# Four one-bank sums, memory attention in row pairs, another order of gates and of weight splits, in an encoder step on one core

## The chip, the cores and the metric

The kernel runs on one core of one Trainium2 chip. The metric is the device time of one execution in microseconds (us). A core has TensorE (PE in the rows: matmuls; PEld is its load of weights), VectorE (DVE), ScalarE (ACT), GpSimd (POOL) and SyncE (SP, which issues most DMAs). TensorE writes its sums to PSUM, eight banks of 512 floats per partition; VectorE and ScalarE read them from there.

## The reference, cut to what matters

One step of a one-layer encoder for 512 prompt rows and 32 sample rows, 544 columns in all in the kernel, width 1024. Three branches are computed from the normalised input, each is projected, gated and added up; then an output projection and a SwiGLU feed-forward part follow:

```python
h = rms_norm(x, norm_mix)
q, k, v, xb, gb, qc = split(h @ w_in)
a_out = diff_attention(q, k, v, ...)                    # 8 heads
b_out = rglru_branch(xb, gb, ...)                       # conv, gates, linear recurrence, gelu
c_out = cross_attention(qc, mem_k, mem_v)               # "memory attention": 4 heads, 256 memory rows
gates = sigmoid(h @ w_gate + b_gate)                    # three of them
merged = gates[0]*(a_out @ w_proj_a) + gates[1]*(b_out @ w_proj_b) + gates[2]*(c_out @ w_proj_c)
x = x + merged @ w_out
h2 = rms_norm(x, norm_ffn)
g_ff, u_ff = split(h2 @ w_ffn_in)
x = x + (silu(g_ff) * u_ff) @ w_ffn_out
```

The memory keys and values, `mem_k` and `mem_v`, are outputs too (`o_mk`, `o_mv`).

## The kernel before

Everything is kept transposed: features on partitions, the 544 rows of the input as columns, in two halves of 272 (`HT`). Each float32 operand is split into a high and a low part (`wh`, `wl` of the weights, `hh`, `hl` of the input), and a product takes three matmuls: high by high, high by low, low by high. ScalarE writes the high part (a split, `split`), VectorE subtracts it for the low part (`LO`).

Weights come in chunks of 1024 x 256. A plain chunk (`gemm`) takes 96 matmuls of 128 x 272. A fast chunk (`seven`) uses seven products, as in Strassen's scheme, of 12 matmuls each: A11, A12, P2, P1, P3, A22, P4, from four quarters of the raw weights and sums of them. A11, P2, P3 and A22 add into one accumulator, `a`; A12 into `c`, P1 and P4 into `b`. `quarters` evacuates: between the products into `a` ScalarE copies the sum so far (events `c11` after A11, `c12` after P2, `u3` after P3), and the next product into `a` waits for that copy. A22 and P4 are held back (`S["pending"]`) and issued by `flush` after A11 of the next chunk.

PSUM holds two two-bank tiles `acc` and four one-bank tiles `side`; a fast chunk takes one half of an `acc` for `a` and two `side` tiles for `c` and `b`, and the scores, transposes and products of memory attention take `side` tiles too.

`load_weights` loads a chunk into one of two `raw` buffers by SP; quarter P1 is then summed in place by an accumulating DMA of GpSimd (event `("raw", i, 1)`), in the feed-forward part also a sum for P3 in `fb`. `split_blocks` writes the splits, chunk after chunk in `ORDER`, into a ring of blocks. It issues A11 of a chunk, then what is late of the chunk before (A22 in the feed-forward part, P4 always, `split_late`), then A12, then VectorE's sum for P2 (`raw<-raw`, which needs the accumulating DMA), P2, P1, P3. A `raw` buffer is given back when P4 is split.

The code is written as many generators that a planner (`Flow`) interleaves by costs that it assumes; each engine then runs its instructions in the order so written, waiting on semaphores. What TensorE does between attention and the output projection follows the list `MID` by hand: `qc` memory queries, `ga`, `gb`, `gc` gates (all four fast), `ya`, `yb`, `yc` branch projections, `x` and `g` the recurrent branch (LRU), and `cross` memory attention, which slips in between by events. `"flush"`, `"cross"`, `"bh"`, `"mh"`, `"lru"` are places where pending products are issued or pools change.

Helper lines in the rows: L254 a ScalarE operation, L267 VectorE tensor by tensor, L276 a fused one, L271 by a scalar, L283 a copy, L318 a DMA, L327 a matmul, L334 a transpose.

## Time and profile before

| | |
|---|---|
| median of 3 runs | 1236.82 us (1236.43 to 1239.05) |
| the profiled execution, own time | 1239.9 us |
| its span, first to last instruction | 1238.1 us |
| mean granted TensorE clock | 0.982 |
| attention | 62 to 310 us |
| last projections of branch a | 310 to 371 us |
| the stage of `MID` up to `yb` 3 | 371 to 745 us |
| `yb`, output projection | 745 to 838 us |
| feed-forward part with its norm | 838 to 1209 us |

The span lies 1.8 us under the execution's own time. A granted clock of 1.00 means 2.4 GHz throughout, a lower mean that TensorE ran a part of the stretch at 1.2 GHz. Starts in the rows count from the span's start.

### The profile page before, as it was taken

How to read it: one execution, taken by the hardware profiler on the slowest of the kernel's cores; microseconds unless marked ns; L12 is line 12 of the kernel's file. 1: busy time of each engine (PE TensorE's matmuls, PEld its weight loads, DVE VectorE, ACT ScalarE, POOL GpSimd, SP SyncE). 2: the span in 40 equal slices, each digit the busy share in tenths (PEclk: the TensorE clock that was granted, in tenths of full speed). 3: DMA queues.
4: the chain of work that ended last, by engine and by line, in shares of the span. 5: the costliest groups of instructions: out<-in, count | busy, mean ns of one | idle time of the engine just before them, and what ended most of it. 6: DMA issues, size and time to landing. Idle time of an engine off the chain costs nothing.

```text
span 1238.1 us, 23076 instructions
## 1 busy us (share of the span) xinstructions
PE 1182.8 (96%) x9200; PEld 1163.1 (94%) x9200; DVE 877.3 (71%) x1861; ACT 585.3 (47%) x1171; POOL 76.4 (6%) x145
## 2 busy tenths in 40 slices
PE   8999999999999997999999689998999999999996
PEld 8899999999999997999999689998999999999996
DVE  6886878786648885475878675578887757756755
ACT  5635454444325554353656653355455525524422
POOL 0002000000000000000111000010111011011001
PEclk9999999999999998999999899998999999999998
DMA  7682343321243443214223133343566556554322
GB/s 263 223 269 97 134 139 116 105 87 58 98 136 103 129 137 111 77 44 145 78 77 112 51 98 143 114 120 95 141 166 138 145 137 168 140 151 120 106 65 73
DMA packets 58875, 151.95 MB, mean 123 GB/s; under 512 B 6632, under 2 KB 18280, under 8 KB 52624
## 3 DMA queue, kind: packets, MB, share of 16 engines
q1 hardware_dynamic: 50560, 135.53, 32.7%
q0 software_dynamic: 8208, 14.95, 7.5%
q8 instruction: 72, 1.18, 0.4%
q14 instruction: 35, 0.29, 0.1%
HBM read 139.52 MB, written 13.68 MB: 124 GB/s over the span
## 4 chain that ended last, share of the span: by engine, by line
PE 85%; DVE 8%; ACT 4%; issue 2%; DMA 1%; SPq 0%; ACTq 0%; DVEq 0%
PE acc L327 65%; PE side L327 19%; DVE wl L267 3%; PE side L334 2%; ACT wh L254 1%; DVE raw L267 1%; DMA raw<-in_w_mem_kv 1%; ACT L L254 0%; ACT t L254 0%; DVE t L267 0%; DVE rst L267 0%; DVE fq L267 0%; DVE x L276 0%; DVE al L267 0%; ACT fq L254 0%
## 5 line engine op out<-in xcount | busy, mean ns | idle before, releaser
L254 ACT ACTIVATE wh<-raw 128x512 fp32r<-128x512 f32 (+2 forms) x357 | 234.5, 669 | 282.6 <-PE acc L327 124.6
L267 DVE TENSOR_TENSOR wl<-raw,wh 128x512 fp32r<-128x512 f32 (+2 forms) x358 | 260.7, 740 | 49.5 <-ACT wh L254 33.4
L327 PE MATMUL acc<-hh,wh 128*128 128x272 f32 x852 | 185.6, 291 | 0.0
L327 PE MATMUL acc<-hl,wh 128*128 128x272 f32 x852 | 184.3, 290 | 0.0
L327 PEld LDWEIGHTS acc<-hh,wh 128*128 128x128 f32 x852 | 137.9, 189 | 0.7 <-ACT fq L254 0.3
L327 PEld LDWEIGHTS acc<-hl,wh 128*128 128x128 f32 x852 | 137.5, 189 | 0.1
L327 PE MATMUL acc<-ah,wh 128*128 128x272 f32 x596 | 127.3, 288 | 0.0
L327 PE MATMUL acc<-al,wh 128*128 128x272 f32 x596 | 127.2, 288 | 0.0
L327 PE MATMUL acc<-hh,wl 128*128 128x272 f32 x852 | 124.7, 291 | 0.1
L327 PE MATMUL acc<-bh,wh 128*128 128x272 f32 (+2 forms) x416 | 98.1, 294 | 17.2 <-ACT t L254 14.5
L327 PEld LDWEIGHTS acc<-hh,wl 128*128 128x128 f32 x852 | 113.3, 189 | 0.6 <-DVE wl L267 0.4
L327 PE MATMUL acc<-bl,wh 128*128 128x272 f32 (+2 forms) x416 | 96.1, 289 | 0.0
L327 PEld LDWEIGHTS acc<-ah,wh 128*128 128x128 f32 x596 | 95.8, 189 | 0.0
L327 PEld LDWEIGHTS acc<-al,wh 128*128 128x128 f32 x596 | 95.5, 188 | 0.0
L327 PEld LDWEIGHTS acc<-bh,wh 128*128 128x128 f32 x416 | 71.5, 190 | 19.7 <-ACT t L254 16.7
L327 PE MATMUL acc<-ah,wl 128*128 128x272 f32 x596 | 84.1, 289 | 0.0
L327 PE MATMUL side<-hh,wh 128*128 128x272 f32 x296 | 77.7, 290 | 2.6 <-DVE t L267 2.1
L327 PEld LDWEIGHTS acc<-ah,wl 128*128 128x128 f32 x596 | 78.7, 189 | 0.0
L267 DVE TENSOR_TENSOR x<-acc,x 128x544 f32<-128x544 f32 (+2 forms) x43 | 29.3, 684 | 69.6 <-PE acc L327 69.6
L327 PE MATMUL side<-hl,wh 128*128 128x272 f32 x296 | 77.1, 288 | 0.0
L327 PEld LDWEIGHTS acc<-bl,wh 128*128 128x128 f32 x416 | 71.3, 190 | 0.0
L327 PE MATMUL acc<-bh,wl 128*128 128x272 f32 (+2 forms) x416 | 63.3, 290 | 0.0
(338 smaller groups left out, 2393.4 us busy)
## 6 DMA issues: line engine op xcount, KB each, us to landing
raw<-in_w_in SPq DMA_DIRECT2D x20, 1024.0 KB, 5.7
raw<-in_w_ffn_in SPq DMA_DIRECT2D x22, 512.0 KB, 4.3
raw<-in_w_ffn_in SPq DMA_DIRECT2D x44, 256.0 KB, 4.8
raw<-in_w_ffn_out SPq DMA_DIRECT2D x12, 768.0 KB, 4.2
raw<-in_w_mem_kv SPq DMA_DIRECT2D x7, 1024.0 KB, 6.5
fb<-in_w_ffn_in SPq DMA_DIRECT2D x22, 256.0 KB, 4.7
raw<-in_w_ffn_in POOLq DMA_DIRECT2D x22, 256.0 KB, 4.3
fb<-in_w_ffn_in POOLq DMA_DIRECT2D x22, 256.0 KB, 5.4
```

Of the source, the lines that this page charges most:

```text
L254: nc.scalar.activation(out, in_, func, scale=scale, bias=bias, accum_out=accum_out)
L267: nc.vector.tensor_tensor(out, a, b, o)
L327: nc.tensor.matmul(out, lhsT=lhsT, rhs=rhs, start=start, stop=stop, skip_group_check=shared)
L334: nc.tensor.transpose(out, in_, ident[:n, :n])
```

## The change

It has seven parts.
1. Between attention and output projection (`switch_sums`) the two two-bank accumulators become four one-bank tiles. `seven` takes its three sums `a`, `c`, `b` from them; `gemm` takes two of them for its two halves, which are evacuated half by half. The `side` tiles are left to memory attention and the LRU.
2. Scores and softmax of memory attention go in pairs of 128 rows (`rows(qp)`): one reduction of 512 in place of two of 256.
3. Memory keys and values are loaded one at a time (`mraw=1`), their high part is cast on ScalarE and no longer on VectorE, and `o_mk`, `o_mv` are written from DRAM to DRAM during attention.
4. `MID` has another order, and gate tiles that are held long get buffers of their own (`HOLD`).
5. `split_blocks` issues VectorE's sum for P2 right after A11, ahead of what is late of the chunk before, and A22 is late everywhere. This holds in the feed-forward part too.
6. Pending products are flushed after a `gemm`'s first tile, or after the fifth piece of one that waits for its operand; `yb` 2 is such a one now.
7. A few small tiles move to other pools.

```diff
+    def switch_sums(one):
+
+        nonlocal accp
+        yield from fl.take(*["acc"] * (2 if one else 4))
+        sums_pool.close()
+        accp = sums_pool.enter_context(tc.tile_pool(name="acc4" if one else "acc2", bufs=2, space=PSUM, reuse_waits="tile"))
+        declare(acc=4 if one else 2)
+        S["one"] = accp if one else None
...
-    MID = [("qc", 0), ("ga", 3), ("qc", 1), ("qc", 2), ("qc", 3), ("gc", 0), ("gc", 1), "flush", "cross",
-           ("yc", 0), ("gc", 2), ("x", 0), ("yc", 1), ("gc", 3), ("yc", 2), ("g", 0), ("x", 1), ("yc", 3), "bh", ("g", 1),
-           ("gb", 0), ("x", 2), ("g", 2), ("x", 3), ("g", 3), ("gb", 1), ("gb", 2), ("gb", 3), ("yb", 2), "mh", ("yb", 3),
-           "lru", ("yb", 0), ("yb", 1)]
+    MID = [("qc", 0), ("qc", 1), ("gc", 0), ("qc", 2), ("qc", 3), ("ga", 3), ("gc", 1), ("gc", 2), "flush", "cross",
+           ("yc", 0), ("x", 0), ("gc", 3), ("yc", 1), ("g", 0), ("x", 1), ("yc", 2), ("yc", 3), "bh", ("g", 1),
+           ("x", 2), ("g", 2), ("x", 3), ("gb", 0), ("g", 3), ("gb", 1), ("gb", 2), ("gb", 3), ("yb", 2), "mh", ("yb", 3), ("yb", 1),
+           "lru", ("yb", 0)]
+
+    HOLD = {("gc", 0): "gt", ("gc", 3): "gt", ("gb", 1): "gt", ("gb", 2): "L", ("gb", 3): "L"}
...
             yield from split((i, "A11"), b4(q[0]))
-            if late is not None:
-                yield from late
-            yield from split((i, "A12"), b4(q[1]))
             yield from fl.get(("raw", i, 1))
-            aside = S.get(("xb", i))
-            p2, a22, p1 = q[0], q[2], q[3]
             VT(p2, p1, q[0], OP.add)
+            while late:
+                yield from late.pop(0)
+            yield from split((i, "A12"), b4(a12))
             yield from split((i, "P2"), b4(p2))
             yield from split((i, "P1"), b4(p1))
-            if aside is not None:
-                yield from split((i, "P3"), b4(aside))
-            else:
-                yield from split((i, "A22"), b4(a22))
-                VT(a22, p2, a22, OP.subtract)
-                yield from split((i, "P3"), b4(a22))
-            late = split_late(i, b4, a22, q[1], p2, aside)
-
-    def split_late(i, b4, a22, a12, p2, aside):
-        if aside is not None:
-            yield from split((i, "A22"), b4(a22))
-        VT(a12, p2, a12, OP.add)
+            if aside is None:
+                VT(p1, p2, a22, OP.subtract)
+            VT(a12, p2, a12, OP.add)
+            yield from split((i, "P3"), b4(p1 if aside is None else aside))
+            late += [split((i, "A22"), b4(a22)), split_last(i, b4, a12, aside)]
+
+    def split_last(i, b4, a12, aside):
         yield from split((i, "P4"), b4(a12))
...
+    def sums():
+
+        if S["one"] is None:
+            yield from fl.take("acc")
+            return slot_tile(accp, [P, 2, 512], F32, "acc")
+        yield from fl.take("acc", "acc")
+        return Halves([slot_tile(S["one"], [P, 512], F32, "acc") for _ in range(2)])
...
-            yield VC(hi, r)
-            t = LO(lo, r, hi)
...
+        yield A(hi, r)
+        t = LO(lo, r, hi)
+        fl.give("mraw", t)
...
+    def bank():
+
+        if S["one"] is None:
+            yield from fl.take("side")
+            return side_tile()[:, :HT], "side"
+        yield from fl.take("acc")
+        return slot_tile(S["one"], [P, 512], F32, "acc")[:, :HT], "acc"
+
     def seven(c, evac, forms):
...
-        yield from fl.take("acc")
-        acc = slot_tile(accp, [P, 2, 512], F32, "acc")
-        a = acc[:, 0, :HT]
+        if S["one"] is None:
+            yield from fl.take("acc")
+            a = slot_tile(accp, [P, 2, 512], F32, "acc")[:, 0, :HT]
+        else:
+            a, _ = yield from bank()
...
-        yield from fl.take("side")
-        S["c", c] = c_ = side_tile()[:, :HT]
-        yield from product(c_, c, "A12", forms, True, True)
+        S["c", c] = yield from bank()
+        yield from product(S["c", c][0], c, "A12", forms, True, True)
```

Three places show what the code does to the engines' queues. (Line numbers of helpers differ by some 23 between the two kernels.)

**Feed-forward part, one chunk boundary.** ScalarE before; `raw_10686` is chunk c, `raw_10808` chunk c+1, `acc_10883` the sum that starts with A11 of chunk c+1, `acc_10759` that of chunk c. The third and fourth rows are the splits of A22 and P4 of chunk c:

```order
L254 ACTIVATE wh_4449<-raw_10808 128x512
L254 ACTIVATE fq_9009<-acc_10759 128x272
L254 ACTIVATE wh_4392<-raw_10686 128x512
L254 ACTIVATE wh_4511<-raw_10686 128x512
L254 ACTIVATE t1_10906<-acc_10883 128x272
L254 ACTIVATE bh_9523<-raw_10808 128x512 x2
```

ScalarE now; `raw_10721` is chunk c, `raw_10843` chunk c+1, `acc_10924` the sum of chunk c+1. The fifth and sixth rows are the splits of A22 and P4 of chunk c:

```order
L277 ACTIVATE wh_4472<-raw_10843 128x512
L277 ACTIVATE bh_9565<-t1_10695 128x544
L277 ACTIVATE fq_9045<-acc_10801 128x272
L277 ACTIVATE t1_10941<-acc_10924 128x272
L277 ACTIVATE wh_4540<-raw_10721 128x512
L277 ACTIVATE wh_4413<-raw_10721 128x512
L277 ACTIVATE bh_9565<-raw_10843 128x512 x2
```

The copy of the sum of A11 of chunk c+1 stood behind the two splits and stands ahead of them now.

VectorE at the same place before (the row `raw_10808<-raw_10808` is the sum for P2 of chunk c+1, the rows `wl<-raw_10686` are the low halves of A22 and P4 of chunk c):

```order
L267 TENSOR_TENSOR wl_4450<-raw_10808,wh_4449 128x512
L267 TENSOR_TENSOR fq_9009<-fq_9009,side_10854 128x272
L267 TENSOR_TENSOR wl_4393<-raw_10686,wh_4392 128x512
L267 TENSOR_TENSOR raw_10686<-raw_10686 128x512
L267 TENSOR_TENSOR fq_9009<-fq_9009,rb_9543 128x272
L267 TENSOR_TENSOR fq_9009<-acc_10759,rb_9543 128x272
L267 TENSOR_TENSOR wl_4512<-raw_10686,wh_4511 128x512
L267 TENSOR_TENSOR bl_9524<-raw_10808,bh_9523 128x512
L267 TENSOR_TENSOR raw_10808<-raw_10808 128x512
```

VectorE now, with `raw_10721` as chunk c and `raw_10843` as chunk c+1:

```order
L290 TENSOR_TENSOR wl_4473<-raw_10843,wh_4472 128x512
L290 TENSOR_TENSOR bl_9566<-t1_10695,bh_9565 128x544
L290 TENSOR_TENSOR fq_9045<-fq_9045,side_10894 128x272
L290 TENSOR_TENSOR fq_9045<-fq_9045,rb_9592 128x272
L290 TENSOR_TENSOR raw_10843<-raw_10843 128x512
L290 TENSOR_TENSOR wl_4541<-raw_10721,wh_4540 128x512
L290 TENSOR_TENSOR wl_4414<-raw_10721,wh_4413 128x512
```

The sum for P2 of chunk c+1 stood behind both low halves of chunk c and stands ahead of them now. TensorE's own order is A11 of chunk c+1, then A22 and P4 of chunk c, in both.

**Gate gb1.** ScalarE before, ahead of the copy of the sum of A11 of gb1 (`t1_8186<-acc_8095`); `raw_7757` is gb1, `raw_7998` gb2, `L` and `brh` belong to the LRU:

```order
L254 ACTIVATE wh_4392<-raw_7998 128x512
L254 ACTIVATE L_8071<-side_8164,brh_91 128x274
L254 ACTIVATE L_8071<-side_8168,brh_91 128x274
L254 ACTIVATE L_8174<-L_8135,spm4_93 128x548
L254 ACTIVATE L_8135<-L_8135,sp4_92 128x548
L254 ACTIVATE wh_4392<-raw_7757 128x512
L254 ACTIVATE L_8184<-L_8174 128x548
L254 ACTIVATE t1_8186<-acc_8095 128x272
```

ScalarE now, ahead of the same copy (`gt_8188<-acc_8160`); `raw_7992` is gb1, `raw_8017` gb2:

```order
L277 ACTIVATE wh_4413<-raw_7992 128x512
L277 ACTIVATE L_8151<-L_8122 128x548
L277 ACTIVATE wh_4413<-raw_7992 128x512
L277 ACTIVATE wh_4472<-raw_7992 128x512
L277 ACTIVATE g2_8183<-t1_8163 128x544
L277 ACTIVATE gt_8188<-acc_8160 128x272
```

The split of A11 of gb2 and that of P4 of gb1, with the LRU's operations between, stood ahead of the copy; the splits of P1 and P3 of gb1 and a `g2` operation stand there now.

**The tail of head 3 of memory attention.** TensorE before (`mh`, `ml` keys by queries `cq`, `ident,ce` transposes of the softmax, `pth`, `ptl` its transpose by the values):

```order
L327 MATMUL side<-mh,cq 128x256 x2
L327 MATMUL side<-ml,cq 128x256
L327 MATMUL side<-mh,cq 128x256 x2
L327 MATMUL side<-ml,cq 128x256
L334 MATMUL side<-ident,ce 128x128 x4
L327 MATMUL side<-pth,mh 128x256
L327 MATMUL side<-ptl,mh 128x256
```

TensorE now, around the transposes of the first half of head 3:

```order
L350 MATMUL acc<-bl,wh 128x272
L350 MATMUL acc<-bh,wl 128x272 x4
L357 MATMUL side<-ident,ce 128x128 x4
L350 MATMUL acc<-bh,wh 128x272
L350 MATMUL acc<-bl,wh 128x272
L350 MATMUL acc<-bh,wh 128x272
L350 MATMUL acc<-bl,wh 128x272
```

and around those of the second half:

```order
L350 MATMUL side<-pth,mlv 128x256
L350 MATMUL acc<-hh,wh 128x272
L350 MATMUL acc<-hl,wh 128x272
L350 MATMUL acc<-hh,wl 128x272 x4
L357 MATMUL side<-ident,ce 128x128 x4
L350 MATMUL side<-pth,mhv 128x256
L350 MATMUL side<-ptl,mhv 128x256
```

Scores, transposes and products followed each other directly; now products of gc2 (`bh` or `hh` by `wh`) stand on both sides of the first transposes and ahead of the second, while the products by the values still follow the second ones directly.

## Rows read from the trace of the kernel before

**Rows 1.** The page: busy us of each engine, share of the span, instructions.
```profile
PE 1182.8 (96%) x9200; PEld 1163.1 (94%) x9200; DVE 877.3 (71%) x1861; ACT 585.3 (47%) x1171; POOL 76.4 (6%) x145
```

**Rows 2.** Windows by stage: length, busy us by engine, granted clock, DMA.
```profile
62.00:310.00 248.00, 248.00 (x1953) 242.70 (x1953) 190.95 (x581) 113.14 (x264) 7.45 (x22) 1.00 0.38 125
371.00:745.00 374.00, 345.69 (x2650) 339.67 (x2649) 268.76 (x510) 202.69 (x409) 23.53 (x67) 0.97 0.31 97
860.00:1200.00 340.00, 335.13 (x2628) 330.31 (x2627) 239.12 (x430) 153.10 (x303) 33.18 (x38) 1.00 0.52 138
```

**Rows 3.** Waits of PE, 371 to 745 us: us in total, times, longest.
```profile
PE acc L327 <- ACT t L254: 14.5, 7, 8.0
```

**Rows 4.** Windows inside the middle stage, columns as before, the clock after POOL.
```profile
464.00:481.00 17.00, 14.89 (x102) 14.07 (x102) 9.96 (x25) 8.38 (x20) 0.86 (x1) 0.90 0.65 189
481.00:497.00 16.00, 11.25 (x56) 9.74 (x57) 8.73 (x24) 4.37 (x12) 0.00 (x0) 0.79 0.04 14
625.00:632.00 7.00, 4.42 (x34) 3.98 (x33) 4.54 (x8) 4.36 (x9) 0.00 (x0) 1.00 0.00 0
705.00:738.00 33.00, 28.91 (x201) 28.25 (x202) 24.79 (x43) 19.38 (x35) 2.65 (x7) 0.89 0.26 73
```

**Rows 5.** Timeline of PE: start, duration, operation, idle before, releaser.
```profile
465.00 0.40 PE L327 MATMUL acc<-bh,wh 128*128 128x272 f32 x1 [2.24 <-ACT t L254]
...
631.11 0.39 PE L327 MATMUL acc<-bh,wh 128*128 128x272 f32 x1 [1.27 <-ACT t L254]
...
704.73 0.60 PE L327 MATMUL acc<-bh,wh 128*128 128x272 f32 x1 [8.02 <-ACT t L254]
...
709.54 0.29 PE L327 MATMUL acc<-bh,wh 128*128 128x272 f32 x1
...
710.54 0.66 PE L327 MATMUL acc<-bh,wl 128*128 128x272 f32 x4
```

**Rows 6.** Timeline of ACT in the feed-forward part.
```profile
886.20 0.63 ACT L254 ACTIVATE wh<-raw 128x512 fp32r<-128x512 f32 x1 [4.18 <-DVE raw L267]
886.73 0.38 ACT L254 ACTIVATE t<-acc 128x272 f32<-128x272 f32 x1
887.01 0.65 ACT L254 ACTIVATE fq<-fq 128x544 f32<-128x544 f32 x1
```

**Rows 7.** Timeline of DVE there, operations back to back.
```profile
884.79 0.68 DVE L267 TENSOR_TENSOR wl<-raw,wh 128x512 fp32r<-128x512 f32 x1
885.40 0.68 DVE L267 TENSOR_TENSOR raw<-raw 128x512 f32<-128x512 f32 x1
```

**Rows 8.** Timeline of ACT ahead of the copy that P2 of gb1 waits for.
```profile
703.21 0.63 ACT L254 ACTIVATE wh<-raw 128x512 fp32r<-128x512 f32 x1 [2.30 <-DVE raw L267]
...
704.29 0.38 ACT L254 ACTIVATE t<-acc 128x272 f32<-128x272 f32 x1
```

**Rows 9.** Timeline of PE at the tail of head 3 of memory attention.
```profile
482.84 0.38 PE L327 MATMUL side<-ml,cq 128*128 128x256 f32 x1 [1.24 <-DVE ml L267]
...
488.49 0.92 PE L334 MATMUL side<-ident,ce 128*128 128x128 f32 x4 [1.25 <-ACT ce L254]
...
494.76 0.38 PE L327 MATMUL side<-pth,mh 128*128 128x256 f32 x1 [0.72 <-ACT pth L254]
...
495.60 0.39 PE L327 MATMUL side<-ptl,mh 128*128 128x256 f32 x1 [0.45 <-DVE ptl L267]
```

**Rows 10.** Timeline of PE in the feed-forward part.
```profile
887.16 1.27 PE L327 MATMUL acc<-m,wh 128*128 128x272 f32 x8 [1.01 <-ACT t L254]
```

**Rows 11.** DMA issues, 886 to 900 us: operation, count, KB each, us to landing.
```profile
raw<-in_w_ffn_in POOLq DMA_DIRECT2D x1, 256.0 KB, 4.3
fb<-in_w_ffn_in POOLq DMA_DIRECT2D x1, 256.0 KB, 5.5
```

**Rows 12.** Timeline of SP's queue: a chunk's loads are issued.
```profile
875.16 0.81 SPq L318 DMA_DIRECT2D raw<-in_w_ffn_in  x2
```

**Rows 13.** Timeline of POOL: its accumulating load is issued.
```profile
880.32 0.86 POOL L424 DMA_DIRECT2D raw<-in_w_ffn_in  x1 [11.37 <-DMA raw<-in_w_ffn_in]
```

More of the change, by code (lines that the diff above doesn't have):

```diff
@@ L604, in gemm @@
                 yield from fl.get(("wh", c, j))
-                yield from fl.take("acc")
-                acc = slot_tile(accp, [P, 2, 512], F32, "acc")
+                acc = yield from sums()
                 ks = range(chunks[c][1])
@@ L641, in gemm @@
             if first:
-                yield from fl.take("acc")
-                accs[i] = slot_tile(accp, [P, 2, 512], F32, "acc")
+                accs[i] = yield from sums()
             left[i].remove((a, k))
@@ L938, in mem_out @@
         fl.set("mem out")
-        yield None
+        yield fl.now + 150000
+        for c in range(4):
+            dma(io["o_mk"][c], mk_d[c], 262144)
+            dma(io["o_mv"].rearrange("(t p) d -> p t d", p=P)[:, :, c * 256:(c + 1) * 256], mv_d[c], 262144)
     def bias_ap(h, rel0, nq, nk):
@@ L1392, in go @@
             gb = t1_tile()
-            t = VC(b2(gb), acc[:, :, :HT])
+            for hf in range(2):
+                t = VC(gb[:, hf * HT:(hf + 1) * HT], acc[:, hf, :HT])
             give_acc(t)
@@ L1553, in cross @@
             if qp == 1:
-                for tg in ("mh", "mh", "ml", "ml"):
-                    fl.give(tg)
+                fl.give("mhv")
+                fl.give("mlv")
             yield fl.now + 100
@@ L1688, in each @@
                     yield A(g[:, cs], src, AF.Tanh, scale=0.5 if cs.start else -0.5, bias=bias(1))
-            g = yield from quarters(i, new if own else new_t1, a, each, -1.0)
+            g = yield from quarters(i, new, a, each, -1.0)
             t = A(g[0], g[0], AF.Tanh, scale=0.5, bias=bias(0))
@@ L1705, in go @@
             g, tag = S["gate", br, n], S["gate tag", br, n]
-            t = VX(b2(g), b2(g), 1.0, acc[:, :, :HT], OP.add, OP.mult)
+            for hf in range(2):
+                s = g[:, hf * HT:(hf + 1) * HT]
+                t = VX(s, s, 1.0, acc[:, hf, :HT], OP.add, OP.mult)
             give_acc(t)
```

243 lines of the change are left out of this document (136 added, 107 removed).

## The prediction

> **What bounds the kernel now.** I read the page's busy times first: TensorE works 1182.8 of 1238.1 us [rows 1], so the time is TensorE's time, and what can be won is where it stands idle or is clocked down. The table by stage says where [rows 2]: from 62 to 310 us (attention) it is busy throughout; in the stage that the change rewrites, 371 to 745 us, it works 345.69 of 374.00 us, so it idles 28.3; from 860 to 1200 us (the feed-forward part) it idles only 340.00 - 335.13 = 4.9. The table of waits of the middle stage [rows 3] puts half of its idle time, 14.5 us in 7 waits, on one kind: a sum waits until ScalarE has copied the part before it out of PSUM (`PE acc <- ACT t`).
>
> The clock row adds a second loss. After the clusters of stalls the granted clock falls: .90 in 464 to 481 us, .79 in 481 to 497, .89 in 705 to 738 [rows 4]. That is 17 x .10 + 16 x .21 + 33 x .11 = 8.7 us of full-clock time; I take 8.5, since a little of it lies in idle time. So the middle stage holds 28.3 + 8.5 = 36.8 us, and no change that leaves the 8966 matmuls as they are can win more there.
>
> Unit prices. Eight matmuls of a product start from 709.54 to 710.54 [rows 5], .125 us apart, so a product of 12 lasts 1.5 us and a chunk of seven products 10.5. A copy of a sum takes ScalarE .38 us, a split of 512 columns .63 [rows 6]; VectorE's steps on 512 columns follow each other .61 apart and last .68 [rows 7].
>
> **The middle stage, part by part.** The new order removes these idle times:
> - 8.02 us before P2 of gb1 and 2.24 before P2 of gc1 [rows 5]. The first is ScalarE's queue: a split ahead of the copy waits 2.30 us for VectorE, and the copy `t<-acc` comes only at 704.29 [rows 8], long after A11 has ended. In the new order that split (P4 of gb1, early) stands behind the copy. Before P2 of gc1 head 2 of memory attention now has matmuls to issue.
> - The tail of head 3 of memory attention, 1.24, 1.25, .72 and .45 [rows 9], where nothing but scores, transposes and products is left to issue. In the new order gate products stand between.
> - The clock that follows both, most of the 8.5.
>
> What takes their place, read from the new order and priced from the rows:
> - Where the stage begins and ends, a new owner of a bank waits for the last reader of a two-bank tile: two waits of about 1.0 (between .72, the shortest wait for a ScalarE copy in the rows [rows 9], and 1.27 [rows 5]), 2.0.
> - Copies that still stand late in ScalarE's queue, in qc0, ga3, gc3, gb0, gb2/gb3. The rows have 1.27 for such a wait [rows 5] and 1.01 [rows 10]; by what stands ahead of each copy I take .75, 1.0, 1.3, 1.5 and 1.0, 5.6 in all (0 to 9).
> - P2 of gb1: no P4 split ahead, but still those of P2, P1 and P3, which hang on VectorE, and a copy to `g2`. Bounds are 1.27 (a wait of gb0 [rows 5]) and 8.02; I take 2.8, as the split with its 2.30 wait now stands behind.
> - The first head's scores: the keys are now loaded through one buffer and cast on ScalarE. It waits for a load (4.3 us for 256 KB [rows 11]), a cast of .63 and a difference of .68, of which qc0's own seven products hide most: bounds 0 and 5.6; I take 2.5.
> - Head 3: the transposes of its second half still have nothing behind them: .45 to 1.25 for each of transposes, copy and difference [rows 9], 2.3 in all, and 1.9 before P3 of gc2, whose copy now queues behind four exponentials (bounds .4 and 2.2): 4.2.
> - Two short half-clock stretches after these, 1.7 each by the deficit of 464 to 481 [rows 4]: 3.4.
>
> Sum 2.0 + 5.6 + 2.8 + 2.5 + 4.2 + 3.4 = 20.5 of 36.8, a **gain of 16.3 us**. With all prices at their lower ends it would be some 30, with all at the upper ones nothing; such luck in six places at once is unlikely, and for the range I use 8 to 22.
>
> Edits that I cost at nothing: the evacuations in halves (some 30 VectorE operations, +.15 each, 4.5 us; VectorE is idle 374.00 - 268.76 = 105 us of the stage [rows 2]; without that cover 4.5); softmax in row pairs (saves VectorE's small operations, off the path); the casts moved to ScalarE (eight of .63 us; it is idle 374.00 - 202.69 = 171 us there); the memory keys and values written out from DRAM during attention, whose TensorE time has no gap [rows 2]; two fewer products after the LRU pool closes (12 us of matmuls of yb0 are left to cover the residual's load). The four one-bank sums let a sum start without waiting for a pair; but each wait above ends with a copy on ScalarE and not with a free bank, so I give them no gain of their own.
>
> **The feed-forward part.** `split_blocks` serves these 22 chunks too, and there the change costs. Of chunk c+1 it now emits A11, then VectorE's sum for P2, and only then the late A22 and P4 of chunk c. The sum for P2 needs the accumulating load, so two things change.
>
> First, ScalarE's queue. At nine chunk boundaries (seven in the first run of twelve chunks, two in the second of six) the copy of A11's sum of chunk c+1 now stands directly ahead of the A22 split of chunk c. TensorE issues A11 of c+1 and then A22 of c. It therefore stops after A11 until the copy and the split are done: about .2 until ScalarE starts, .28 from a copy to the instruction behind it and .63 for a split [rows 6], and .05 until TensorE starts (the copy ends at 886.73 + .38 = 887.11 [rows 6], TensorE goes on at 887.16 [rows 10]; the .2 is an estimate, from this .05 upwards): 1.15 us each. Before, the split was far ahead there.
>
> Second, the loads. A raw buffer is free once P4 of its chunk is split. The load starts at 875.16 [rows 12], GpSimd's accumulate at 880.32 [rows 13], and lands 4.3 later [rows 11]: 9.5 us. In the new order the low half of A22, that of P4 and so the next load come behind VectorE's sum: .61 + .61 + .69 after the landing. The loop is 9.5 + 1.9 = 11.4, and 12.6 if the landing took the 5.5 of the accumulate beside it [rows 11], against 10.5 us of matmuls. Before, the late splits hung on no landing, and a lead of several products could be used up slowly: such a stall shows singly, 1.01 us [rows 10].
>
> Both together give one period, the larger of 10.5 + 1.15 and 11.4; I take 11.7, a stall of 1.2 at each of nine places, 10.8 us (bounds 0, and 9 x 2.1 = 19 from the 12.6). About 2 of the 4.9 us idle now stay. The **feed-forward part loses** 10.8 + 2 - 4.9 = **7.9 us**.
>
> [...]
>
> **Sum.** 1239.9 us (the profiled execution) - 16.3 + 7.9 = 1231.5. That execution is 3.1 us above the median of the runs, 1236.8, so 1228.4 by the runs: I forecast **1228.5 us**, 0.7% faster. A measurement tells 0.2%, 2.5 us, from no change.
>
> **Rivals.**
> - *The feed-forward stalls don't come.* If loads land early enough and the copy is taken at once, only the middle stage counts: 1236.8 - 16.3 = 1220.5, with a better middle stage 1215. For it: 1.15 is small, and the stalls now seen there are few. Against it: the order of ScalarE's queue is fixed, and 9.5 + 1.9 exceeds 10.5.
> - *Slower: the stalls of the feed-forward part take the clock with them.* Nine regular stalls of 1.2 us, each followed by a half-clock stretch that costs 1.7: 15.3 more, 1243.8. It decides from five of the nine on, where the gain of 8.4 is gone (8.4 / 1.7 = 4.9), and from seven on it is measurably slower. For it: clusters of stalls of 1.24 and 1.25 did bring .79 [rows 4, 9]. Against it: the wait of 1.27 at 631.11 [rows 5], with TensorE busy 4.42 of 7 us around it, left it at 1.00 [rows 4], and here the stalls lie 11 us apart. The Trainium skill ("TensorE: Matmul & The Clock Gate", "A second HAM failure mode") tells of a kernel that cycles through PSUM banks, idles briefly between groups of matmuls and sees its clock swing, which is this rival; the clock of 1.00 at 625 to 632 speaks against it.
> - *The wait before P2 of gb1 stays.* ScalarE still has a split that waits for VectorE, and the LRU's `g2`, ahead of the copy. With 8.0 in place of 2.8, and the clock loss of some 3.4 behind it: 8.6 more, 1237, no change.
>
> **How the numbers follow.** Forecast .50 (1222 to 1235), no stalls in the feed-forward part .17, clock lost there .17, gb1's wait stays .16. The range 1216 to 1243 reaches into the first two rivals and holds the third. In that order, faster takes .44 + .17 + 0 + .01 = .62, no change .04 + 0 + .02 + .08 = .14, slower .02 + 0 + .15 + .07 = .24.
>
> **What would show it.** In the profile after: TensorE idle in the middle stage near 17 us in place of 28.3 and its clock .98 or better; before P2 of gb1 under 4; in the feed-forward part a row of TensorE waits near 1.2 us, one a chunk, released by ScalarE's split of raw weights (`ACT wh` or `bh`), nine of them, idle time there near 13 us, clock 1.00. Wrong if these waits are under .5 or over 2, if the clock drops between them, or if a wait over 4 us shows up in the middle stage at a place that I counted as small, the first head's scores above all.

## The result and the profile after

The changed kernel takes 1218.92 us (median of four runs, 1216.19 to 1221.86) against 1236.62 of the kernel before on the same chip: a ratio of 0.9854, with an interval of 0.9827 to 0.9882. That is 17.7 us faster. The forecast was 1228.5, a gain of 8.3; the time lies near the lower end of the forecast range, 1216 to 1243, and the gain is more than twice the forecast one. The profiled execution took 1221.86 us, its span 1220.1.

First the page of after: busy time by engine, and the granted clock over 40 slices of the span. TensorE works 6.8 us less than in [rows 1] for the same 9200 matmuls. Of the slices but the last one shows less than .9, that from 793 to 824 us, where the norm begins. A fall to half clock for 3.4 of a slice's 30.5 us leaves .94 and still shows as 9, so the two falls in the middle stage, below, aren't seen in this row.

```profile
PE 1176.0 (96%) x9200; PEld 1159.1 (95%) x9200; DVE 872.7 (72%) x1857; ACT 590.8 (48%) x1183; POOL 76.3 (6%) x145
PEclk9999999999999999999999999989999999999998
```

The windows of after by stage, columns as in [rows 2]: the middle stage without its ends, the feed-forward part, and 20 us around P2 of gb1.

```profile
371.00:735.00 364.00, 353.57 (x2769) 349.84 (x2769) 270.48 (x510) 210.55 (x426) 23.29 (x67) 0.99 0.32 99
840.00:1180.00 340.00, 328.72 (x2592) 325.22 (x2591) 233.09 (x418) 151.41 (x299) 33.34 (x38) 1.00 0.51 136
680.00:700.00 20.00, 17.00 (x121) 16.78 (x122) 16.33 (x30) 14.78 (x26) 1.83 (x5) 0.91 0.24 66
```

The middle stage idles 364.00 - 353.57 = 10.4 us where it idled 28.3 [rows 2]. The feed-forward part idles 340.00 - 328.72 = 11.3 us, where it idled 4.9, at a clock of 1.00.

Windows of two kernels don't hold the same work. TensorE executes 9200 matmuls in both, and the changed order keeps the stages at the same counts, so I cut all traces at the same matmul numbers. In us, from the start of one matmul to the start of another:

| stretch (matmul numbers) | before | after | difference |
|---|---|---|---|
| start and attention (to 2475) | 321.9 | 319.9 | -2.0 |
| middle stage to the end of the output projection (to 6250) | 515.7 | 491.9 | -23.8 |
| norm (to 6314) | 14.4 | 17.3 | +2.9 |
| feed-forward part (to 9166) | 368.8 | 373.4 | +4.6 |
| the rest | 8.9 | 9.1 | +0.2 |

The differences make -18.1 (-18.0 by the spans; the rows are rounded). The middle stage was forecast at -16.3, the feed-forward part at +7.9; the norm had no term. The -2.0 of the start belongs to no edit that I know of: among the other runs this stretch varies from 318.9 to 324.7.

**The feed-forward part.** The table of waits of TensorE in after, 838 to 1190 us (us in total, times, longest):

```profile
PE acc L350 <- ACT wh L277: 5.0, 5, 1.0
PE acc L350 <- ACT bh L277: 4.0, 4, 1.0
PE acc L350 <- DVE wl L290: 1.5, 3, 1.0
PE acc L350 <- DVE bl L290: 0.5, 1, 0.5
```

Nine waits (five `wh`, four `bh`) of 1.00 us are the nine places of the forecast. One of them in the timeline of TensorE:

```profile
875.47 0.29 PE L350 MATMUL acc<-al,wh 128*128 128x272 f32 x1
875.60 0.66 PE L350 MATMUL acc<-ah,wl 128*128 128x272 f32 x4
877.26 1.27 PE L350 MATMUL acc<-m,wh 128*128 128x272 f32 x8 [1.00 <-ACT wh L277]
...
889.03 1.27 PE L350 MATMUL acc<-m,wh 128*128 128x272 f32 x8 [1.00 <-ACT wh L277]
```

and what ScalarE does there:

```profile
874.85 0.40 ACT L277 ACTIVATE fq<-acc 128x272 f32<-128x272 f32 x1 [1.04 <-PE acc L350]
876.29 0.40 ACT L277 ACTIVATE t<-acc 128x272 f32<-128x272 f32 x1 [1.04 <-PE acc L350]
876.59 1.66 ACT L277 ACTIVATE wh<-raw 128x512 fp32r<-128x512 f32 x3
```

A11 of the next chunk ends at 876.26. ScalarE, idle until then, copies its sum (876.29), then makes the split of A22 (876.59), and TensorE goes on at 877.26. This is the chain of the forecast, link by link.

**The norm.** Its 2.9 us are another matter. TensorE's wait for the sum of squares (`sqa`), before and after:

```profile
841.00 0.61 PE L327 MATMUL side<-ones_d,sqa 128*128 128x1 f32 x4 [1.91 <-DVE sqa L267]
815.98 0.80 PE L350 MATMUL side<-cols,sqa 128*128 128x1 f32 x3 [2.63 <-DVE sqa L290]
```

VectorE after; its sum for P2 of a feed-forward chunk (`raw<-raw`) now stands ahead of the last sum of squares:

```profile
814.60 0.69 DVE L290 TENSOR_TENSOR raw<-raw 128x512 f32<-128x512 f32 x1
815.21 0.72 DVE L290 TENSOR_TENSOR sqa<-sqa,t 128x544 f32<-128x544 f32 x1
```

The wait is 0.72 longer, and the half clock about it lasts 10.2 us in place of 6.8 (mean clock .72 from 813 to 831 us, .81 in the same 18 us of before, 838 to 856). In run 1 below both are as before, 1.91 and .81.

**The middle stage.** The waits of TensorE in after, 371 to 745 us. The 14.5 us of [rows 3] have become 2.5, and a new kind, copies into the held gate tiles (`gt`), has 4.4:

```profile
PE acc L350 <- ACT gt L277: 4.4, 2, 3.1
PE acc L350 <- ACT t L277: 2.5, 2, 1.5
PE side L350 <- ACT pth L277: 1.4, 1, 1.4
PE acc L350 <- ACT L L277: 0.6, 1, 0.6
```

The longest, before P2 of gb1, in the timeline of TensorE (before it was 8.02 [rows 5]):

```profile
682.44 0.40 PE L350 MATMUL acc<-bh,wh 128*128 128x272 f32 x1 [3.06 <-ACT gt L277]
```

and on ScalarE, where a split ahead of the copy still waits for a sum of VectorE:

```profile
680.93 0.63 ACT L277 ACTIVATE wh<-raw 128x512 fp32r<-128x512 f32 x1 [2.46 <-DVE raw L290]
681.47 0.64 ACT L277 ACTIVATE g<-t 128x544 f32<-128x544 f32 x1
682.01 0.38 ACT L277 ACTIVATE gt<-acc 128x272 f32<-128x272 f32 x1
```

How long splits stand in ScalarE's queue and wait for VectorE sets the two kernels clearly apart. The table of waits of ScalarE, rows of raw weights released by VectorE, before, 371 to 745 us:

```profile
ACT wh L254 <- DVE raw L267: 59.7, 29, 8.9
```

and after, the same stretch:

```profile
ACT wh L277 <- DVE raw L290: 21.0, 11, 4.8
```

The forecast doesn't use this row. While a split waits there, all that is behind it on ScalarE waits too, the copies that release TensorE among it.

### The profile page after: what moved, and what is told of

The parts are those of the page before. It is cut to its first block, busy times and chain, and to the rows that moved or that the text cites. A ratio compares the mean times of both kernels' runs of the same rounds, so it can differ in the third digit from the quotient of the medians.

```text
span 1220.1 us, 23097 instructions
## 1 busy us (share of the span) xinstructions
PE 1176.0 (96%) x9200; PEld 1159.1 (95%) x9200; DVE 872.7 (72%) x1857; ACT 590.8 (48%) x1183; POOL 76.3 (6%) x145
## 4 chain that ended last, share of the span: by engine, by line
PE 82%; DVE 6%; ACT 5%; DMA 4%; issue 2%; SPq 0%; POOL 0%; DVEq 0%; ACTq 0%; POOLq 0%
PE acc L350 66%; PE side L350 15%; DMA raw<-in_w_ffn_in 2%; PE side L357 2%; DVE wl L290 1%; ACT L L277 1%; ACT wh L277 1%; DMA raw<-in_w_mem_kv 1%; DVE L L299 1%; SPq L341 0%; DMA memT<-in_mem 0%; DMA raw<-in_w_gate 0%; DVE raw L290 0%; DVE g L299 0%; ACT m L277 0%
## 5 line engine op out<-in xcount | busy, mean ns | idle before, releaser
L350 PE MATMUL acc<-hh,wh 128*128 128x272 f32 x956 | 213.4, 291 | 0.4 <-DVE t L290 0.2
L350 PE MATMUL acc<-hl,wh 128*128 128x272 f32 x956 | 210.8, 289 | 0.0
L350 PEld LDWEIGHTS acc<-hh,wh 128*128 128x128 f32 x956 | 157.0, 189 | 1.7 <-DVE t L290 0.4
L350 PEld LDWEIGHTS acc<-hl,wh 128*128 128x128 f32 x956 | 156.5, 188 | 0.1
L350 PE MATMUL acc<-hh,wl 128*128 128x272 f32 x956 | 141.3, 290 | 0.0
L350 PEld LDWEIGHTS acc<-hh,wl 128*128 128x128 f32 x956 | 127.5, 188 | 0.1
L350 PE MATMUL acc<-bh,wh 128*128 128x272 f32 (+2 forms) x468 | 111.7, 293 | 8.5 <-ACT gt L277 4.4
L350 PE MATMUL acc<-bl,wh 128*128 128x272 f32 (+2 forms) x468 | 110.0, 290 | 0.0
L350 PEld LDWEIGHTS acc<-bh,wl 128*128 128x128 f32 x468 | 63.9, 189 | 0.7 <-DVE wl L290 0.7
L290 DVE TENSOR_TENSOR raw<-raw 128x512 f32<-128x512 f32 x83 | 56.0, 688 | 11.8 <-DMA raw<-in_w_ffn_in 10.6
```

Of the source, the lines that this page charges most:

```text
L290: nc.vector.tensor_tensor(out, a, b, o)
L350: nc.tensor.matmul(out, lhsT=lhsT, rhs=rhs, start=start, stop=stop, skip_group_check=shared)
```

## The experiments

After the first comparison three explanations of the larger gain stood. One: the order of splits, in which VectorE's sums are issued ahead, frees ScalarE's queue in the middle stage too (where I had priced it in the feed-forward part alone). Two: the four one-bank sums. Three: the new order of gates or the buffers of the held gate tiles. All ratios are to the kernel before, with their intervals; stage lengths are counted as in the table above, from one profiled execution of each kernel. The runs were made on four chips, where the kernel before has medians of 1236.4 to 1238.2 us, so a step of 2 us between medians of two chips says little. The runs stand in the order in which they were made.

**Run 1: after, in the feed-forward part the late splits ahead of the sum.**

```
             yield from split((i, "A11"), b4(q[0]))
+            while late and aside is not None:
+                yield from late.pop(0)
             yield from fl.get(("raw", i, 1))
             VT(p2, p1, q[0], OP.add)
```

> The changed kernel, but in the feed-forward part the late splits (A22, P4 of the chunk before) stand ahead of the wait for the accumulating load and of VectorE's sum for P2 again, as before the change. Theory A (the change has two parts of opposite sign: the middle stage gives some 24 us, the feed-forward split order takes some 6 back): the nine TensorE waits of 1.00 us there vanish, idle time of TensorE in the feed-forward part falls from 11.3 to about 5 us, 1213 us (1210 to 1215). Rival (the loads bound this part anyway, the idle time only moves to other waits): idle time stays at 9 or more, 1217 to 1221 us.

Measured: 1207.11 us, 0.9754 (0.9738 to 0.977), 11.8 less than after. The feed-forward part fell from 373.4 to 361.0, the norm from 17.3 to 14.4, the middle stage stayed (491.0). The waits of TensorE, 826 to 1190 us, hold none of the nine:

```profile
PE acc L350 <- ACT t L277: 1.3, 2, 0.9
PE acc L350 <- ACT fq L277: 0.8, 2, 0.5
PE side L350 <- DVE rsy L299: 0.3, 1, 0.3
```

So the loss there is the place of the late splits, and the part is 7.8 us shorter than even before, whose TensorE showed only 4.9 us idle. The run moves the late splits ahead of the copy and ahead of the sum's wait for the load, so it doesn't tell my two reasons apart; the timeline above fits the first alone.

**Run 2: before, with the new order of splits and nothing else** (`split_plain`, `split_blocks` and `split_last` of the change). Its core:

```
             yield from split((i, "A11"), b4(q[0]))
-            if late is not None:
-                yield from late
-            yield from split((i, "A12"), b4(q[1]))
...
             VT(p2, p1, q[0], OP.add)
+            while late:
+                yield from late.pop(0)
+            yield from split((i, "A12"), b4(a12))
...
+            VT(a12, p2, a12, OP.add)
```

> The kernel before, with the new order of splits alone (sum for P2 ahead of the late splits, A22 late everywhere); old order of the middle stage, old banks, single rows. Theory A: the feed-forward part loses 6 us through nine waits of about 1 us, the middle stage moves by less than 5 us: 1243 us (1239 to 1247). Rival (the split order is itself what shortens the middle stage, since raw buffers and ScalarE come free in another order): TensorE's idle time in the middle stage falls by 8 us or more, the whole at 1236 or below.

Measured: 1230.42, 0.9948 (0.9931 to 0.9965). The middle stage fell from 515.7 to 501.9, by 13.8; norm and feed-forward part rose by 8.1. The profiled execution was the slowest of this kernel, 1237.21 us; run 6, whose edits in the middle stage are the same, has 504.1 there, a gain of 11.6. So of the change's 23.8 in the middle about half is an edit to which the forecast gave no term there. ScalarE's waits for VectorE's sums, 371 to 745 us, fell from 59.7 to half:

```profile
ACT wh L254 <- DVE raw L267: 28.5, 12, 4.7
```

**Run 3: after, with two-bank sums throughout** (both calls left out).

```
         fl.spawn(h_forms())
-        yield from switch_sums(True)
         yield from after_attention(HEAD[GA:])
...
-        yield from switch_sums(False)
```

> The changed kernel without the switch to four one-bank sums: two two-bank accumulators and side tiles as before, all else as changed. Theory A (waits end with a copy on ScalarE, not with a free bank): within 2 us of the changed kernel, 1217 to 1221 us. Theory B (the one-bank sums are what frees the middle stage): 1226 us or more, with TensorE waits released by the evacuation of side or acc tiles.

Measured: 1223.03, 0.9886 (0.9869 to 0.9904): 4.1 more than after by the medians, intervals overlapping; the middle stage 2.2 longer. What the banks are worth in the new order of gates isn't clear of the noise.

**Run 4: after, in the order of gates of before** (only `yb` 1 stays ahead of the LRU's end).

```
-    MID = [("qc", 0), ("qc", 1), ("gc", 0), ("qc", 2), ("qc", 3), ("ga", 3), ("gc", 1), ("gc", 2), "flush", "cross",
...
-           ("x", 2), ("g", 2), ("x", 3), ("gb", 0), ("g", 3), ("gb", 1), ("gb", 2), ("gb", 3), ("yb", 2), "mh", ("yb", 3), ("yb", 1),
+    MID = [("qc", 0), ("ga", 3), ("qc", 1), ("qc", 2), ("qc", 3), ("gc", 0), ("gc", 1), "flush", "cross",
...
+           ("gb", 0), ("x", 2), ("g", 2), ("x", 3), ("g", 3), ("gb", 1), ("gb", 2), ("gb", 3), ("yb", 2), "mh", ("yb", 3), ("yb", 1),
```

> The changed kernel with the order of the middle stage as before (ga3 second, gc2 and gc3 behind yc0 and yc1, gb0 ahead of x2); only yb1 stays ahead of the place where the LRU pool closes. Theory A (the order carries most of the middle stage's gain): a long wait before P2 of gb1 (4 us or more) and the bare tail of head 3 (4 us or more) come back, 1234 us (1228 to 1240). Theory B: 1222 us or less.

Measured: 1219.18, 0.9854 (0.9837 to 0.9871), the time of after. The new order of gates, on which I had put most of the gain, is worth nothing net. It has two halves of opposite sign. The stretch of gates gb (matmuls 5030 to 5444) takes 55.6 us here and 61.1 in after. In the new order that stretch holds most of gb0, which the old order has ahead of it; cut at matmul 4714, up to which both orders have done the same matmuls, the stretch to 5444 takes 95.7 us here and 100.8 in after, and the middle stage ahead of it 293.3 here and 288.6 in after. There the old order waits once, by the timeline of TensorE, for memory attention's transposes:

```profile
481.08 1.09 PE L357 MATMUL side<-ident,ce 128*128 128x128 f32 x4 [5.55 <-DVE ce L294]
```

**Run 5: after, with the late splits first in every fast chunk** (run 1 without its condition).

```
+            while late:
+                yield from late.pop(0)
             yield from fl.get(("raw", i, 1))
             VT(p2, p1, q[0], OP.add)
```

> As the first run (late splits ahead of the wait and of the sum for P2), but in every fast chunk, in the middle stage too. Theory B now (what shortens the middle stage is that the sums of VectorE are issued ahead of the splits that need them, so that ScalarE's queue is not held up by a split that waits; whether the late splits stand before or behind the sum for P2 does not matter there): within 3 us of the first run, 1204 to 1210 us. Rival (the place ahead of the late splits is what helps in the middle stage): the middle stage grows by 5 us or more, 1212 us or more.

Measured: 1204.77, 0.9736 (0.9715 to 0.9756), 2.3 less than run 1 with overlapping intervals. The middle stage is 488.4.

**Run 6: before, with the order of splits of the change and run 1's rule in the feed-forward part** (the edits of runs 2 and 1).

> The kernel before with the new order of splits, and in the feed-forward part the late splits ahead of the sum for P2; old order of the middle stage, old banks, single rows. Theory B (the order of splits works by itself, in both stages): 12 us under the second run, 1218 us (1215 to 1221), the feed-forward part 361 us long as in the first run. Rival (its good effect in the feed-forward part needs the other parts of the change): 1224 us or more.

Measured: 1218.12, 0.9842 (0.9823 to 0.9862). This leaves out banks, row pairs, casts, order of gates and held tiles, and is as fast as the whole change: middle stage 504.1, feed-forward part 361.3.

**Run 7: after, with memory attention one row block at a time** (`cross` with the softmax of before).

```
-        def rows(qp):
+        def rows(i):
...
-            e = slot_tile(cr, [P, 2, NMEM], F32, "ce")
+            e = slot_tile(cr, [P, NMEM], F32, "ce")
...
+            yield from soft_rows(s_[:, :NMEM], e, True)
```

> The changed kernel with scores and softmax of memory attention one row block at a time, as before; the loads and casts of memory keys and values stay as changed. The row pairs' own share is open: of the 24 us of the middle stage the split order has 14 and the banks 2 to 4, so at most some 6 are left for it and the loads. If the pairs have them: 1223 to 1226 us, with more waits on scores and softmax. If not: within 2 us of the changed kernel, 1217 to 1221.

Measured: 1218.42, 0.9844 (0.9824 to 0.9864): no difference from after. This holds for the new order of gates; in the old order single rows weren't tried with the rest of the change.

**Run 8: run 1 with gb0 back at its earlier place.** It takes the better half of each order of run 4.

```
-           ("x", 2), ("g", 2), ("x", 3), ("gb", 0), ("g", 3), ("gb", 1),
+           ("gb", 0), ("x", 2), ("g", 2), ("x", 3), ("g", 3), ("gb", 1),
```

> The first run with gb0 ahead of x2 again, as in the kernel before, and the rest of the new order. In the fourth run this half of the old order had waits of 1.1 and 1.3 us where the new one has .8, 1.0, 3.1, .6 and .5, while the new first half had less than the old one. Theory B: 3 us less than the first run, 1204 us (1202 to 1206). Rival (the waits come back in another place, as ScalarE has the same work): 1206 to 1210.

Measured: **1202.84 us**, 0.9718 (0.9698 to 0.9738), 4.3 less than run 1; the stretch from matmul 4714 to 5444 fell from 101.2 to 95.6. Its median is 35.4 us under that of the kernel before on the same chip and 16.1 under that of after.

**Run 9: run 5 with the same move** (the edits of runs 5 and 8).

> Late splits ahead of the sum for P2 in every fast chunk, and gb0 ahead of x2 as in the kernel before: the two edits that helped on top of the first run, together. If they add up: 1207.1 - 2.3 - 4.3 = 1200.5 us (1198 to 1203). If the waits that one removes return through the other: 1203 us or more.

Measured: 1202.98, 0.9725 (0.9711 to 0.9739). I had expected 1200.5; the 2.3 of run 5 didn't come again, so late splits first outside the feed-forward part gain nothing that holds.

**Run 10: run 4 with two-bank sums** (the edit of run 3). It asks whether the banks help in the old order.

> The fourth run (old order of the middle stage, all else changed) without the four one-bank sums. The run with the split order alone has 66.4 us for the stretch of the gates gb, the fourth run 55.6, at the same order of the gates. Theory C (with the old order the one-bank sums are what removes these 10.8 us, a part of the change that I had put at nothing): the stretch goes back to 63 to 67 us, 1227 to 1231 us in all. Rival (the buffers of their own for the held gate tiles, HOLD, remove them): 1219 to 1221 us.

Measured: 1217.48, 0.9849 (0.9831 to 0.9867), 1.7 less than run 4. The theory that the one-bank sums remove the 10.8 us falls: leaving them out costs 4.1 in one order and gives 1.7 in the other, both with overlapping intervals.

**Run 11: run 4 without buffers of their own for three of the held gate tiles.**

```
-    HOLD = {("gc", 0): "gt", ("gc", 3): "gt", ("gb", 1): "gt", ("gb", 2): "L", ("gb", 3): "L"}
+    HOLD = {("gb", 2): "L", ("gb", 3): "L"}
```

> The fourth run with the held gate tiles in the buffers that they had before (gb2, gb3 in L, all others among the four t1). Theory C: within 2 us of the fourth run, 1217 to 1221 us. Rival (HOLD): the stretch of the gates gb back at 63 us or more, 1227 to 1231 us, with ScalarE's copy of gb1 late for want of a t1 tile.

Measured: 1228.29, 0.9934 (0.992 to 0.9947), 9.1 more than run 4. In the timeline of TensorE, P2 of gb1 waits long again:

```profile
690.78 0.60 PE L350 MATMUL acc<-bh,wh 128*128 128x272 f32 x1 [5.44 <-ACT t L277]
```

and ScalarE's timeline shows why: the copy, now into a shared `t1` tile, comes behind the LRU's operations that free such a tile.

```profile
682.14 0.63 ACT L277 ACTIVATE wh<-raw 128x512 fp32r<-128x512 f32 x1 [3.31 <-DVE raw L290]
...
689.62 0.64 ACT L277 ACTIVATE g<-g 128x544 f32<-128x544 f32 x1
690.34 0.40 ACT L277 ACTIVATE t<-acc 128x272 f32<-128x272 f32 x1
```

In run 4, with the buffer, the same piece of ScalarE's timeline has the copy right behind the split:

```profile
680.61 0.63 ACT L277 ACTIVATE wh<-raw 128x512 fp32r<-128x512 f32 x1 [3.31 <-DVE raw L290]
681.15 0.64 ACT L277 ACTIVATE g<-t 128x544 f32<-128x544 f32 x1
681.70 0.38 ACT L277 ACTIVATE gt<-acc 128x272 f32<-128x272 f32 x1
```

The same split waits the same 3.31 us ahead of both. The copy starts 8.20 us after the split in one (690.34 - 682.14) and 1.09 us after it in the other.

**Run 12: run 5 with VectorE's two sums back beside the splits that need them.**

```
             yield from split((i, "A11"), b4(q[0]))
-            yield from fl.get(("raw", i, 1))
-            VT(p2, p1, q[0], OP.add)
             while late:
                 yield from late.pop(0)
             yield from split((i, "A12"), b4(a12))
+            yield from fl.get(("raw", i, 1))
+            VT(p2, p1, q[0], OP.add)
...
-            VT(a12, p2, a12, OP.add)
...
+    def split_last(i, b4, a12, p2, aside):
+        VT(a12, p2, a12, OP.add)
         yield from split((i, "P4"), b4(a12))
```

> The fifth run (late splits first everywhere, 1204.8 us) with VectorE's sums put back to where the kernel before had them: that for P2 behind the split of A12, that for P4 right ahead of its split. Theory B (issued late, a sum holds up ScalarE's queue and with it the copies that TensorE waits for): ScalarE waits for VectorE's sums (wh or bh from raw) 40 us or more again in the feed-forward part, that part is 369 us long in place of 361, 1213 us or more in all. Rival (only the place of the late splits matters): 1203 to 1207 us.

Measured: 1232.53, 0.9965 (0.995 to 0.9979), 27.8 more than run 5, from two instructions a chunk that are issued later. The middle stage rose by 20.8 (488.4 to 509.2), the feed-forward part by 7.7, to 368.9, the 368.8 of before. ScalarE's waits in run 12, 371 to 745 us:

```profile
ACT wh L277 <- DVE raw L290: 59.8, 31, 5.3
```

and in run 5:

```profile
ACT wh L277 <- DVE raw L290: 17.8, 12, 4.8
```

They come near the 59.7 and the 21.0 of before and after. In the feed-forward part (838 to 1190 us, `wh` and `bh` together) they rose from 25.4 in run 5 to 82.8, where before has 81.9. The first explanation holds; which of the two sums counts for more isn't shown.

**Run 13: after, with memory attention's casts on VectorE again.**

```
-        yield A(hi, r)
+        yield VC(hi, r)
         t = LO(lo, r, hi)
```

> The changed kernel with the casts of the memory keys and values on VectorE again, as before. I had put the move at nothing: 1217 to 1221 us. Rival (VectorE is late at the tail of memory attention, so the move is part of the gain): 1222 us or more.

Measured: 1221.72, 0.9873 (0.9854 to 0.9892), 2.8 more than after with overlapping intervals; the middle stage is 492.2, as in after. Inconclusive, and small either way.

**Run 14: after, with gb1's gate tile alone back in `t1`.**

```
-    HOLD = {("gc", 0): "gt", ("gc", 3): "gt", ("gb", 1): "gt", ("gb", 2): "L", ("gb", 3): "L"}
+    HOLD = {("gc", 0): "gt", ("gc", 3): "gt", ("gb", 2): "L", ("gb", 3): "L"}
```

> The changed kernel, new order, with only gate gb1 among the four t1 tiles again (gc0, gc3 keep their own buffers, without which this order runs out of t1 tiles). Under the old order the buffers' 9 us showed as a wait of 5.4 us before P2 of gb1. If the new order owes gb1's buffer the same: 1223 us or more, that wait at 4 us or more in place of nothing. If gb0, now late, is what holds gb1 up in the new order: 1217 to 1221 us.

Measured: 1224.83, 0.9906 (0.9883 to 0.9929), 5.9 more than after. The wait before P2 of gb1, which I had expected at 4 us or more here and at nothing in after, is the same in both, 3.05 and 3.06. The loss stands later, where a sum for gb1 waits for a copy (1.58 us) and the next product for VectorE:

```profile
681.75 0.39 PE L350 MATMUL acc<-bh,wh 128*128 128x272 f32 x1 [3.05 <-ACT t L277]
...
696.00 0.39 PE L350 MATMUL acc<-hh,wh 128*128 128x272 f32 x1 [3.09 <-DVE t L290]
```

The waits of TensorE, 371 to 745 us, have 7.1 us released by copies into `t`, 3.3 by VectorE's `t` and 1.4 by copies into `gt`, 11.8 in place of the 7.1 of these rows in after (2.5, 0.2 and 4.4):

```profile
PE acc L350 <- ACT t L277: 7.1, 4, 3.0
PE acc L350 <- DVE t L290: 3.3, 2, 3.1
```

So the buffer pays in the new order too, at another place. With all three tiles in `t1` this order can't be planned, and there is no time for it: it holds more gate tiles at once than `t1` has.

The runs line up as a ladder from before to after, by the medians:

| kernel | us | step |
|---|---|---|
| before | 1236.6 | |
| with the new order of splits (run 2) | 1230.4 | -6.2 (in its profile, the slowest of this kernel: start +2.7, middle -13.8, norm and feed-forward +8.1) |
| with banks, row pairs, casts and the rest, but old order of gates and old tiles (run 11) | 1228.3 | -2.1 |
| with the held tiles (run 4) | 1219.2 | -9.1 |
| with the new order of gates (after) | 1218.9 | -0.3 |

The loads one at a time, the copies from DRAM to DRAM, the flushes and the moved small tiles (parts 3, 6 and 7) were not taken out by themselves; they are in the step of -2.1.

## Why the prediction was wrong

**The step that failed** is the sum of the middle stage, 16.3 us, and in it what the parts were taken to do. The stage gave 23.8, and this is 7.5 of the 9.6 by which the profiles missed the forecast (18.0 in place of 8.4); the start has 2.0 more, and norm and feed-forward part together lost 0.4 less than forecast. In the prediction's own terms 5.4 of the 7.5 are waits that it sized too large, of the 20.5 that were to take the place of the old ones. The sign that it named, TensorE idle near 17 us in the stage, came out at 10.4. What the runs show in their place: the order of splits and the held tiles, which have no term in the sum, carry most of the stage's gain, 11.6 to 13.8 us (runs 2 and 6) and 7.6 (498.1 in run 11 to 490.5 in run 4).

*The order of splits was priced on one side only.* "`split_blocks` serves these 22 chunks too, and there the change costs", the prediction says of the feed-forward part, and gives the edit no gain of its own in the middle stage. Runs 2 and 6 have 13.8 and 11.6 us of gain there from it, run 12 has 20.8. The row that would have told it is ScalarE's own: 59.7 us of waits for VectorE's sums. I followed TensorE's waits to the copy (`ACT t`) and in one case to the split ahead of it [rows 8], and treated that as a feature of one place. It was the rule of the stage: a split in ScalarE's queue that waits for a sum which VectorE has just been given.

*The end of the wait before P2 of gb1 was put down to the order of gates.* The wait is 8.02 in before. With the order of splits alone it is 5.61 (runs 2 and 6), by TensorE's timeline of run 2:

```profile
696.68 0.59 PE L327 MATMUL acc<-bh,wh 128*128 128x272 f32 x1 [5.61 <-ACT t L254]
```

With all of the change but the new order of gates and the three held tiles it is 5.44 (run 11), and with the held tiles too it is gone (run 4). The new order brings 3.06 of it back (after), and with gb0 at its old place it is gone again (run 8). So the order of gates did the opposite of what the prediction gave it credit for; the splits took 2.4, and in the old order the held tiles, 9.1 us of the time, took the rest. Within the new order the reading was right: P4's split stands behind the copy, and the split of P3, which waits 2.46 us for VectorE, ahead of it, so 2.8 came out as 3.06. The rival in which this wait stays has no run at its 8.0; 5.61 and 5.44 come nearest.

*What takes their place was mis-sized, mostly upwards.* The idle times in the trace of after against the terms: transitions of the banks 0.68 and 0.84, 1.5 for 2.0; late copies 1.38 (gc3), 1.01 (gb0) and 0.56 (gb2), with 0.69 of waits for VectorE behind the last, 3.6 for 5.6, and none in qc0 and ga3; the first head's scores 0.20 for 2.5; the tail of head 3 for 4.2 is these waits in TensorE's timeline, with one of 0.14 besides, 3.3 in all:

```profile
481.80 0.39 PE L350 MATMUL acc<-bh,wh 128*128 128x272 f32 x1 [1.48 <-ACT t L277]
...
490.63 0.38 PE L350 MATMUL side<-pth,mhv 128*128 128x256 f32 x1 [1.36 <-ACT pth L277]
...
491.36 0.43 PE L350 MATMUL side<-ptl,mhv 128*128 128x256 f32 x1 [0.34 <-DVE ptl L290]
```

The clock's 3.4 came out in this execution: two stretches of 3.4 us at half clock, from 491.6 and from 682.7, each half lost. The first of them is luck: it is missing in runs 1, 3, 7 and 14, which have the same two waits ahead of it (below). The terms make 15.1 for 20.5. The 2.1 us still open between 36.8 - 15.1 = 21.7 and 23.8 I put down to steps that are slow without showing as idle (below); no run isolates them in this stage. (The prediction's 8966 matmuls are 9200 in [rows 1]; no term uses the number.)

**What was right, and what was luck.** The chain of the feed-forward part was right: nine waits at the nine places, seven and two, as they were worked out (1.15 forecast; start to start it is 877.26 - 875.97 = 1.29, where 875.97 is the start of the last of the four at 875.60, less the pitch of .126: 1.16). After and the eight runs with this order there all have nine waits of 1.00, and run 1 removes them. Whether the loads' loop of 11.4 us would have set the period by itself stays open. That the 7.9 comes so near to the 7.5 of norm and feed-forward part is luck. The feed-forward part itself lost 4.6 (its length is 371.0 to 373.9 in these nine kernels, against 368.8), since the stalls of before, which the forecast took off at their idle time of 4.9, had cost more (below); the other 2.9 are the norm's, for which there was no term.

The rival with the clock is out: nine such stalls, 11.8 to 13.1 us apart within the two runs of chunks, left the granted clock at 1.00. In the nine kernels with these stalls it fell once, for 3.4 us in run 2, where a wait of 1.30 us for VectorE follows one of the nine by 2.6 us. The swing of the clock that the Trainium skill tells of ("TensorE: Matmul & The Clock Gate", "A second HAM failure mode"), from short idle times between groups of matmuls, does not come with these stalls. The rival without feed-forward stalls named almost the time that came (1220.5), but its stalls did come.

Of the edits taken at nothing, the banks (runs 3 and 10), the row pairs in the new order (run 7) and the casts (run 13) are nothing that these runs can tell from it. The held tiles were wrongly not named among them. In the old order the row pairs may cost: their transposes wait 5.5 us at the tail of head 3 (runs 4, 10 and 11), where single rows wait 1.26 (run 2); these kernels differ in more than that, so it isn't shown.

## What to carry to other kernels

Where TensorE waits for a copy on another engine, look at that engine's own waits over the whole stage, not only at the instruction ahead of the one copy: 31 to 42 us fewer of them on ScalarE were worth 12 to 21 us of TensorE in the middle stage (runs 2, 6 and 12). Issue what the other engine must wait for early, and the instruction that hangs on it late. The sum of these waits is not the cost by itself, though: in the feed-forward part after has 7.0 us of them and run 1 has 21.0, and run 1 is 12.4 us shorter there. What counts is what stands behind the instruction that waits. So put copies and splits into the queue in the order in which TensorE needs them, as run 1 does with the split of A22 and the copy. A tile that is held long is better taken from a pool that no recurrent chain shares (9.1 us for three tiles in run 11, 5.9 for one in run 14).

## What the runs showed of the chip that was not expected

Idle time understates a stall. A wait of 1.00 in the table costs 1.16 us from start to start, and the feed-forward part of before, with 4.9 us idle, is 7.5 us longer than that of run 6 (368.8 and 361.3), which does the same matmuls. Part of the difference, some 3 us, are 30 matmuls that start .20 to .25 apart in place of .126 (six in run 6) and are all counted as busy, so a stage that shows 335.13 of 340.00 us busy at full clock [rows 2] held more to win than its 4.9.

The same waits don't always bring the same clock. Two places alone in the middle stage of after were followed by half clock: the 3.06 us before P2 of gb1, and the 1.36 with the 0.34 behind it. The wait of 1.48 us nine us earlier was not (the eight matmuls behind it start .12 to .13 apart, from 482.03 on), nor were the nine of 1.00 in the feed-forward part. The 3.06 was followed by half clock in all six kernels that have it (after, runs 1, 5, 7, 13 and 14). The 1.36 with the 0.34 was in after and run 8, but not in runs 1, 3, 7 and 14. Windows of after around the 1.48 and around the 1.36, and of run 1 around the 1.36, the clock after POOL:

```profile
481.00:489.00 8.00, 7.07 (x56) 6.83 (x56) 3.65 (x9) 4.63 (x12) 0.00 (x0) 1.00 0.63 221
488.00:498.00 10.00, 8.30 (x53) 7.86 (x52) 3.02 (x5) 3.58 (x6) 1.01 (x3) 0.83 0.29 68
488.00:498.00 10.00, 8.30 (x66) 7.87 (x65) 3.71 (x6) 4.31 (x8) 1.01 (x3) 1.00 0.45 112
```

In the last two TensorE shows the same 8.30 us busy, but 53 matmuls in after and 66 in run 1. What decides whether the clock falls there stays open.
